# Weight pieces, x tiles and merged tiles placed at multiples of 256 bytes

## The chip, the cores and the metric

The kernel runs on one core of a Trainium2 chip. The metric is device time in microseconds (us) of one execution. Four compute engines matter here: TensorE (PE in the profile; its weight loads have a row of their own, PEld), VectorE (DVE), ScalarE (ACT) and GpSimd (POOL). SyncE (SP) issues the loads from device memory.

## The reference

Two layers, each of 256 tokens by 2048 features, all in float32. Of a layer, this is what costs time:

```python
h = jnp.einsum('bsd,dc->bsc', x, w_in)          # 2048 x 16396 columns
qa, ka, va, za, qb, kb, vb, zb, f_logit, g_logit = jnp.split(h, SPLIT_POINTS, axis=-1)
...
up_a = jnp.einsum('bsw,wd->bsd', out_a * jax.nn.silu(za), w_up_a)   # 1536 x 2048
up_b = jnp.einsum('bsw,wd->bsd', out_b * jax.nn.silu(zb), w_up_b)
gates = jax.nn.sigmoid(g_logit + b_gate)
g_a, g_b = gates[..., :D_MODEL], gates[..., D_MODEL:]
y = jnp.einsum('bsd,de->bse', g_a * up_a + g_b * up_b, w_out)       # 2048 x 2048
return layer_norm(DEEPNORM_ALPHA * x + y, ln_g, ln_b)
```

Between the projections stand two attentions of 12 heads each (one dilated with rotary positions, one with forget gates) over 256 tokens; they are small beside the projections.

## The kernel before, in words

Features lie on the 128 partitions, tokens along the free axis. To keep float32 accuracy every operand of a projection is split into two float32r parts, a high and a low one (`split`, L62: ACT writes the rounded high part, DVE the remainder). A product then takes two matmuls per contraction tile: the weights' high part against both parts of the activations (512 columns, L153), and the weights' low part against the activations' high part (256 columns, L157). The text calls these two matmuls one pair. Each matmul has a weight load of 128 columns of its own.

The work is a list of units. A unit is one tile of 128 weight columns against all 256 tokens, 16 contraction tiles long (12 for the up projections). It is cut into two pieces of 8 (or 6) contraction tiles. For each piece `load_raw` issues one load into one of 7 raw buffers, and `Piece.prep` splits it into one of 6 `w` buffers, which are used in turn; pieces are prepared about four ahead of the products.

Three kinds of activations are the moving operand of such units: `x` (L103 `x_at`), `gated` (12 tiles; the attention outputs) and `merged` (16 tiles that live in the 20 slots of 2 KB of the pool `s2`). In the units that make the attention values (`v_mm`, L328 on) the roles are turned round: slices of `x` are the stationary operand and both parts of the weights move (L340: 512 columns, L341: 256).

A layer runs in this order: 12 mixer pairs (six per attention branch; each one is six units on x for q, k and z, one value unit, and the attention of two heads, whose small products stand between the units), then units for the gates (on x) and the up projections (on gated) in turn, then 16 units of the output projection (on merged), then the normalisation, which writes x for the next layer. TensorE's program is this list in order.

Where the operands lie is what the change touches. Tiles of a pool stand one behind the other in each partition. In the built program:

- A `w` buffer holds [2, 1072] floats, that is 8576 bytes or 33.5 times 256. The first begins at byte 56576 (221 times 256), so buffers 0, 2 and 4 begin at a multiple of 256 and buffers 1, 3 and 5 lie 128 bytes behind one. The low part begins 4288 bytes (16.75 times 256) behind the high one: 192 bytes behind a multiple of 256 in buffers 0, 2, 4, and 64 behind one in 1, 3, 5. Slices of a piece are 512 bytes apart, so this holds for all of them. The text calls buffers 0, 2, 4 the even ones.
- Each x tile holds [part, contraction tile, 256 tokens] and begins at a multiple of 256. A 512-column moving operand is two runs of 1 KB, 2 KB apart.
- `gated` tiles begin at multiples of 256, and their 512 columns are one run of 2 KB.
- The tile `f_t` of 96 bytes stands in front of `s2`, so every slot of `s2`, and with them `merged`, begins 96 bytes behind a multiple of 256; the 512 columns are one run.

Of the kernel before, what the change touches and what calls it, by code (L numbers as in the profile page):

```python
# [10 lines left out]
F32 = mybir.dt.float32  # L11
F32R = mybir.dt.float32r
AF = mybir.ActivationFunctionType
ALU = mybir.AluOpType
# [4 lines left out]
S = 256  # L19
HD = 128  # L20
HEADS = 12
# [11 lines left out]
SLOT = KT // 4 * (NV + HEADS)  # L33


@with_exitstack
def trunk(ctx: ExitStack, tc: tile.TileContext, xt, w_st, w_v, w_vf, w_up, w_o,
# [17 lines left out]

# [1 line left out]
    def load_raw(ap, n):  # L57
# [8 lines left out]
    class Piece:  # L66
        """Some contraction tiles of one unit's weights."""

# [4 lines left out]
        def prep(self):  # L73
            n = len(self.kts) * self.w
            raw = load_raw(self.ap, n)
            self.t = wp.tile([128, 2, SLOT], F32R, name="w", tag="w", bufs=6)
            split(self.t[:, 0, :n], self.t[:, 1, :n], raw)
# [5 lines left out]
    class Unit:  # L83
        """One tile of weight columns against all tokens."""

# [5 lines left out]
        def cut(self, chunks):  # L91
            """Cut into pieces of the given numbers of contraction tiles."""
            self.pieces = []
            k = 0
            for n in chunks:
                self.pieces.append(Piece(self, self.ap[:, k * self.w:(k + n) * self.w], range(k, k + n), self.w))
                k += n
            self.pieces[0].first = True
            self.pieces[-1].last = True
# [3 lines left out]
    def x_at(kt):  # L103
        return xs[kt // 2][:, :, kt % 2]

    def load_x(k0, n):
        raw = load_raw(xt[:, k0:k0 + n, :].rearrange("p a b -> p (a b)"), n * S)
        for i in range(n // 2):
            x = xs[k0 // 2 + i]
            split(x[:, 0].rearrange("p a b -> p (a b)"), x[:, 1].rearrange("p a b -> p (a b)"),  # L110
                  raw[:, 2 * i * S:2 * (i + 1) * S])

# [13 lines left out]
    def keep_warm(n):  # L126
        """Products nobody reads: an idle TensorE falls to half its clock."""
        p = psc.tile([128, 2 * S], F32, name="pw", tag="po")
        for _ in range(n):
            nc.tensor.matmul(p, warm[:, :128], warm, start=True, stop=True)  # L130
# [16 lines left out]
    def stat_mm(acts, ps, kt_n, halves=2):  # L147
        """Products with both parts of the activations, and of their high part with the weights' low part."""
        def mm(kt, w):
            a = acts(kt)  # L150
            first, last, o = kt == 0, kt == kt_n - 1, ps()[:, :S]
            if halves == 2:
                nc.tensor.matmul(ps(), w[:, 0], a, start=first, stop=False)  # L153
            else:
                nc.tensor.matmul(o, w[:, 0], a[:, 0], start=first, stop=False)  # L155
                nc.tensor.matmul(o, w[:, 0], a[:, 1], start=False, stop=False)  # L156
            nc.tensor.matmul(o, w[:, 1], a[:, 0], start=False, stop=last)  # L157
        return mm

    def fold(dst, ps, scale=1.0):  # L160
        """dst = scale * (sum of the two halves of a bank)"""
        c = att.tile([128, S], F32, name="c", tag="c", bufs=3)
        nc.scalar.activation(c, ps[:, S:], AF.Copy, scale=scale)  # L163
        if scale == 1.0:
            nc.vector.tensor_tensor(dst, ps[:, :S], c, op=ALU.add)  # L165
        else:
            nc.vector.scalar_tensor_tensor(dst, ps[:, :S], scale, c, op0=ALU.mult, op1=ALU.add)

    def pair_units(aps, acts, nk, done, scale=1.0, put=None, halves=(2, 2)):
        """Two column tiles, whose results come side by side."""  # L170
        st = {}
        ps = {}

        def before(i):
            ps[i] = mm_tile()

        def after(i):
            if put:
                put(i, ps[i])
            else:  # L180
                if i == 0:
                    st["p"] = slot("p")
                fold(st["p"][:, i], ps[i], scale)
            if i == 1:
                done(st.get("p"))

        return [Unit(ap, nk, 128, stat_mm(acts, lambda i=i: ps[i], nk, halves[i]),
                     before=lambda i=i: before(i), after=lambda i=i: after(i))
                for i, ap in enumerate(aps)]

# [1 line left out]
    def build_layer(l):  # L192
# [9 lines left out]
        def forget(psv):  # L202
            f = att.tile([128, 2, HEADS], F32, name="f_t", tag="f_t", bufs=1)
            for t in range(2):
                nc.vector.tensor_copy(f[:, t], psv[t][:, NV:NV + HEADS])
            lf["f"] = f
# [31 lines left out]
        def attention(br, p, st):  # L238
            """Stages of the attention of one pair of heads."""
            hs = [dict(), dict()]  # L240
# [184 lines left out]

        # output projection, residual, statistics (of four times the residual sum)
        ln = {"s": []}

        def residual(j2):
            u = slot("u")  # L430
            r = big.tile([128, 2, S], F32, name="gated", tag="gated", bufs=HEADS)
            x = xs[j2].bitcast(F32)
            nc.gpsimd.tensor_tensor(u, x[:, 0], x[:, 1], op=ALU.add)  # L433
            if j2 == 0:
                ln["u"] = u
            else:
                nc.vector.scalar_tensor_tensor(r, u, alpha4, ln["c"][:, None, :].to_broadcast([128, 2, S]),
                                               op0=ALU.mult, op1=ALU.subtract)
            ln[j2] = r

        def add_stats(r, sl):
            """Sums over the feature tiles of the shifted values and of their squares."""
            if not ln["s"]:
                ln["s"] = [slot("lns") for _ in range(2)]
                nc.scalar.activation(ln["s"][1], r, AF.Square)
                nc.vector.tensor_copy(ln["s"][0], r)
                return
            sq = slot("sq")
            nc.scalar.activation(sq[:, sl], r[:, sl], AF.Square)
            for a, b in zip(ln["s"], (r, sq)):  # L450
                nc.vector.tensor_tensor(a[:, sl], a[:, sl], b[:, sl], op=ALU.add)

        def add_in(dst, ps):
            """dst += both halves of a bank"""
            c = att.tile([128, S], F32, name="c", tag="c", bufs=3)
            nc.scalar.activation(c, ps[:, S:], AF.Copy)
            nc.vector.tensor_tensor(dst, dst, ps[:, :S], op=ALU.add)
            nc.vector.tensor_tensor(dst, dst, c, op=ALU.add)
# [18 lines left out]
        def last_tiles():  # L477
# [3 lines left out]
            def first(ps):  # L481
                add_in(r[:, 0], ps)
                add_stats(r, slice(0, 1))
                for a in ln["s"]:
                    nc.vector.tensor_tensor(a[:, 0], a[:, 0], a[:, 1], op=ALU.add)
                # brings in the table set that the statistics need
                t = sm.tile([128, 1], F32, name="t", tag="t", bufs=1)
                nc.scalar.activation(t, ln["s"][1][:, 0, :1], AF.Sqrt)

            def second(ps):  # L490
# [3 lines left out]
                pst = psc.tile([128, 2, 2], F32, name="pst", tag="pt")  # L494
                # the sums share one bank, which the first product clears
                for n, (a, i) in enumerate([(ln["s"], 0), ((r, sq), 1)]):
# [11 lines left out]
        def spread(v, name):  # L508
            """A value per token, on every partition."""
            p = psc.tile([128, S], F32, name=name, tag="s", bufs=2)  # L510
# [30 lines left out]
        def ln_apply(j2):  # L541
            r, x = ln[j2], xs[j2]
            g, b = ([t[:, l * KT + 2 * j2 + i:l * KT + 2 * j2 + i + 1] for i in range(2)] for t in (lng, lnb))
            if j2 == 0 and not final:
                for i in range(2):
                    nc.vector.tensor_tensor(r[:, i], r[:, i], ln["pa"], op=ALU.mult)
                    nc.scalar.activation(x[:, 0, i], r[:, i], AF.Identity, scale=g[i], bias=b[i])
                    nc.vector.tensor_scalar(r[:, i], r[:, i], g[i], b[i], op0=ALU.mult, op1=ALU.add)
                    ins = nc.vector.tensor_tensor(x[:, 1, i], r[:, i], x[:, 0, i].bitcast(F32),  # L549
                                                  op=ALU.subtract)  # L550
            else:
# [11 lines left out]
                if not final:  # L563
                    nc.scalar.activation(x[:, 0], r, AF.Copy)
                    ins = nc.vector.tensor_tensor(x[:, 1], r, x[:, 0].bitcast(F32), op=ALU.subtract)
            if not final:
# [18 lines left out]

# [1 line left out]
    units, jobs, interleaved, norms = [], {}, set(), {}  # L587
# [32 lines left out]
    for g in order:  # L620
        done += len(g)
        n = number[id(g[0].unit)]
        if g[0].first and n in norms:
            # the normalisation comes before what is prepared for later
            stats, apply = norms[n]
# [105 lines left out]
```

## Time and profile before

| | |
|---|---|
| median of 3 runs | 1997.46 us (1996.6 to 1997.53) |
| the profiled execution, first to last instruction | 1996.8 us |
| PE busy | 1974.5 us (99%), 11449 matmuls |
| DVE busy | 1270.7 us (64%) |
| ACT busy | 988.3 us (49%) |
| POOL busy | 75.9 us (4%) |

The profiled execution is 0.66 us shorter than the median, so a sum made against the profile's 1996.8 us is taken to the median by adding 0.66. A matmul's duration in the profile holds its latency, and matmuls overlap; what one costs on TensorE is read from the distance of its start to the start of the next.

### The profile page before, as it was taken

To read this page: it belongs to the slowest core of one execution; us is meant where nothing else is said; L and a number is where in the kernel's file an instruction comes from. 1 tells how busy PE (TensorE), PEld (TensorE's weight loads), DVE (VectorE), ACT (ScalarE), POOL (GpSimd) and SP (SyncE) were. 2 spreads that over 40 slices of the span, in tenths; PEclk is the share of its full clock that TensorE was granted. 3 is DMA by queue.
4 is the path that set the end of the run, shared out by engine and by line. 5 is a ranking of instruction groups with operands and counts; after the bars stand their busy time and mean duration, and the time that the engine had idled before them with its cause. 6 is when DMAs were issued, how large, how long until landed. Compare 5 with 4: busy or idle time off the path is not lost.

```text
span 1996.8 us, 29718 instructions
## 1 busy us (share of the span) xinstructions
PE 1974.5 (99%) x11449; PEld 1733.9 (87%) x11449; DVE 1270.7 (64%) x1896; ACT 988.3 (49%) x1555; POOL 75.9 (4%) x69
## 2 busy tenths in 40 slices
PE   9999999999999999999999999999999999999997
PEld 7888888889888888888888888888898888888886
DVE  7666665555555555668777666655555555556686
ACT  5444445454544445554455444445454444445544
POOL 0000000001000000001200000000010000000022
PEclk9999999999999999999999999999999999999998
DMA  8655555666556555565455555566666555556651
GB/s 305 198 172 178 177 160 174 189 196 213 183 177 182 178 168 178 182 200 189 158 169 178 170 180 174 163 181 183 205 200 185 184 178 176 168 173 194 204 182 60
DMA packets 107766, 362.74 MB, mean 182 GB/s; under 512 B 12368, under 2 KB 15592, under 8 KB 107624
## 3 DMA queue, kind: packets, MB, share of 16 engines
q1 hardware_dynamic: 106600, 357.68, 57.7%
q0 software_dynamic: 1024, 3.17, 0.6%
q8 instruction: 89, 1.46, 0.3%
q14 instruction: 53, 0.43, 0.1%
HBM read 358.68 MB, written 2.12 MB: 181 GB/s over the span
## 4 chain that ended last, share of the span: by engine, by line
PE 97%; DVE 1%; DMA 1%; ACT 0%; issue 0%; DVEq 0%; ACTq 0%
PE mm L153 53%; PE mm L157 27%; PE mm L340 8%; PE mm L341 4%; PE ps_s L247 1%; PE po L276 1%; PE pt L267 1%; DMA raw<-xt 1%; PE ps_s L246 1%; PE po L277 1%; PE mm L336 0%; PE mm L337 0%; PE mm L338 0%; DVE gated L557 0%; PE mm L156 0%; PE mm L155 0%
## 5 line engine op out<-in xcount | busy, mean ns | idle before, releaser
L153 PE MATMUL mm<-x,w 128*128 128x512 f32 x3328 | 1183.4, 399 | 8.0 <-DVE x L549 4.8
L64 DVE TENSOR_TENSOR w<-raw,w 128x1024 fp32r<-128x1024 f32 (+3 forms) x713 | 839.6, 1182 | 461.7 <-ACT w L63 460.3
L63 ACT ACTIVATE w<-raw 128x1024 fp32r<-128x1024 f32 (+3 forms) x713 | 716.9, 1007 | 471.3 <-issue 225.2
L157 PE MATMUL mm<-x,w 128*128 128x256 f32 x3328 | 932.2, 280 | 0.2 <-DVE w L64 0.2
L153 PEld LDWEIGHTS mm<-x,w 128*128 128x128 f32 x3328 | 626.9, 189 | 151.6 <-issue 5.1
L157 PEld LDWEIGHTS mm<-x,w 128*128 128x128 f32 x3328 | 627.8, 189 | 2.6 <-DVE w L64 1.4
L163 ACT ACTIVATE c<-mm 128x256 f32<-128x256 f32 x320 | 122.2, 384 | 453.4 <-PE mm L157 423.8
L153 PE MATMUL mm<-gated,w 128*128 128x512 f32 x768 | 267.5, 393 | 0.0
L340 PE MATMUL mm<-w,x 128*128 128x512 f32 x704 | 245.6, 392 | 0.0
L165 DVE TENSOR_TENSOR p<-mm,c 128x256 f32<-128x256 f32 x252 | 106.6, 424 | 187.1 <-ACT c L163 186.6
L157 PE MATMUL mm<-gated,w 128*128 128x256 f32 x768 | 213.9, 279 | 0.0
L341 PE MATMUL mm<-w,x 128*128 128x256 f32 x704 | 197.0, 280 | 0.0
L153 PEld LDWEIGHTS mm<-gated,w 128*128 128x128 f32 x768 | 144.2, 188 | 32.9
L153 PE MATMUL mm<-merged,w 128*128 128x512 f32 x480 | 168.9, 395 | 0.0
L340 PEld LDWEIGHTS mm<-w,x 128*128 128x128 f32 x704 | 132.0, 187 | 29.6
L157 PEld LDWEIGHTS mm<-gated,w 128*128 128x128 f32 x768 | 143.9, 187 | 0.0
L157 PE MATMUL mm<-merged,w 128*128 128x256 f32 x512 | 143.5, 280 | 0.0
L341 PEld LDWEIGHTS mm<-w,x 128*128 128x128 f32 x704 | 132.7, 189 | 0.0
L153 PEld LDWEIGHTS mm<-merged,w 128*128 128x128 f32 x480 | 90.1, 188 | 21.6 <-DVE merged L64 0.6
L157 PEld LDWEIGHTS mm<-merged,w 128*128 128x128 f32 x512 | 96.2, 188 | 0.1
L433 POOL TENSOR_TENSOR u<-x 128x512 f32<-128x512 f32 x16 | 31.6, 1977 | 609.4 <-DVE merged L64 487.4
L256 ACT ACTIVATE z<-z,s 128x128 f32<-128x128 f32 x96 | 42.3, 444 | 0.0
(129 smaller groups left out, 939.4 us busy)
## 6 DMA issues: line engine op xcount, KB each, us to landing
raw<-w_st SPq DMA_DIRECT2D x410, 512.0 KB, 3.7
raw<-w_up SPq DMA_DIRECT2D x128, 384.0 KB, 3.2
raw<-w_v SPq DMA_DIRECT2D x88, 512.0 KB, 4.3
raw<-w_o SPq DMA_DIRECT2D x64, 512.0 KB, 3.7
raw<-w_vf SPq DMA_DIRECT2D x8, 536.0 KB, 4.0
nb<-cum POOLq DMA_DIRECT2D x12, 256.0 KB, 4.6
raw<-w_st SPq DMA_DIRECT2D x9, 256.0 KB, 5.9
yt<-gated SPq DMA_DIRECT2D x8, 256.0 KB, 2.1
```

The lines of the kernel that those rows point to most:

```text
L63: nc.scalar.activation(hi, src, AF.Copy)
L64: nc.vector.tensor_tensor(lo, src, hi.bitcast(F32), op=ALU.subtract)
L153: nc.tensor.matmul(ps(), w[:, 0], a, start=first, stop=False)
L157: nc.tensor.matmul(o, w[:, 1], a[:, 0], start=False, stop=last)
L163: nc.scalar.activation(c, ps[:, S:], AF.Copy, scale=scale)
L165: nc.vector.tensor_tensor(dst, ps[:, :S], c, op=ALU.add)
L246: nc.tensor.matmul(ps[:, 0], q[:, :128], k[:, :128], start=True, stop=True)
L247: nc.tensor.matmul(ps[:, 1:3].rearrange("p a b -> p (a b)"), q[:, 128:], k, start=True, stop=True)
L256: nc.scalar.activation(z[:, sl], z[:, sl], AF.Exp, scale=-1.0, bias=s4[:, c:c + 1], accum_out=s4[:, 2 + c:3 + c])
L340: nc.tensor.matmul(o, xh, w, start=first, stop=False)
L341: nc.tensor.matmul(o[:, :NV], xl, w[:, 0], start=False, stop=last)
L433: nc.gpsimd.tensor_tensor(u, x[:, 0], x[:, 1], op=ALU.add)
```

## The change

The low part of a `w` buffer begins `PART` = 1088 floats (4352 bytes, 17 times 256) behind the high part, and a buffer is 8704 bytes (34 times 256), so that both parts of all six buffers begin at multiples of 256. An x tile holds [contraction tile, part, 256 tokens]: it still begins at a multiple of 256, and a 512-column operand is one run of 2 KB. `f_t` is given 256 bytes, so that `s2`, and with it `merged`, begins at a multiple of 256. The stationary slices of x in the value units stay at multiples of 256. In the value units the moving weights are, as before, one run of each part.

```diff
 SLOT = KT // 4 * (NV + HEADS)
 
+PART = (SLOT + 63) // 64 * 64
...
             raw = load_raw(self.ap, n)
-            self.t = wp.tile([128, 2, SLOT], F32R, name="w", tag="w", bufs=6)
+            self.t = wp.tile([128, 2, PART], F32R, name="w", tag="w", bufs=6)
             split(self.t[:, 0, :n], self.t[:, 1, :n], raw)
...
     def x_at(kt):
-        return xs[kt // 2][:, :, kt % 2]
+        return xs[kt // 2][:, kt % 2]
...
             x = xs[k0 // 2 + i]
-            split(x[:, 0].rearrange("p a b -> p (a b)"), x[:, 1].rearrange("p a b -> p (a b)"),
-                  raw[:, 2 * i * S:2 * (i + 1) * S])
+            split(x[:, :, 0], x[:, :, 1],
+                  raw[:, 2 * i * S:2 * (i + 1) * S].rearrange("p (a b) -> p a b", a=2))
...
         def forget(psv):
-            f = att.tile([128, 2, HEADS], F32, name="f_t", tag="f_t", bufs=1)
+            f = att.tile([128, 64], F32, name="f_t", tag="f_t", bufs=1)
+            f = f[:, :2 * HEADS].rearrange("p (a b) -> p a b", a=2)
...
-            nc.gpsimd.tensor_tensor(u, x[:, 0], x[:, 1], op=ALU.add)
+            nc.gpsimd.tensor_tensor(u, x[:, :, 0], x[:, :, 1], op=ALU.add)
...
-                    nc.scalar.activation(x[:, 0], r, AF.Copy)
-                    ins = nc.vector.tensor_tensor(x[:, 1], r, x[:, 0].bitcast(F32), op=ALU.subtract)
+                    nc.scalar.activation(x[:, :, 0], r, AF.Copy)
+                    ins = nc.vector.tensor_tensor(x[:, :, 1], r, x[:, :, 0].bitcast(F32), op=ALU.subtract)
```

No instruction is added, removed or moved on any engine, and each waits for what it waited for. Fifteen ACT and fifteen DVE instructions that write x get two runs of 256 elements instead of one of 512. ACT's program at its start, before (x_81 to x_88 are the eight x tiles):

```order
L63 ACTIVATE x_81<-raw 128x512
L63 ACTIVATE w<-raw 128x256 x3
L63 ACTIVATE x_82<-raw 128x512
L63 ACTIVATE w<-raw 128x256 x3
L63 ACTIVATE x_83<-raw 128x512
```

And of the change, the same place:

```order
L65 ACTIVATE x_81<-raw 128x2x256
L65 ACTIVATE w<-raw 128x256 x3
L65 ACTIVATE x_82<-raw 128x2x256
L65 ACTIVATE w<-raw 128x256 x3
L65 ACTIVATE x_83<-raw 128x2x256
```

Only the shape of the written tile differs.

## Rows read from the trace of the kernel before

**Rows 1.** The page: busy time by engine, and the granted clock in 40 slices.

```profile
PE 1974.5 (99%) x11449; PEld 1733.9 (87%) x11449; DVE 1270.7 (64%) x1896; ACT 988.3 (49%) x1555; POOL 75.9 (4%) x69
...
PEclk9999999999999999999999999999999999999998
```

**Rows 2.** The page: the chain that ended last, shares by engine and by line.

```profile
PE 97%; DVE 1%; DMA 1%; ACT 0%; issue 0%; DVEq 0%; ACTq 0%
PE mm L153 53%; PE mm L157 27%; PE mm L340 8%; PE mm L341 4%; PE ps_s L247 1%; PE po L276 1%; PE pt L267 1%; DMA raw<-xt 1%; PE ps_s L246 1%; PE po L277 1%; PE mm L336 0%; PE mm L337 0%; PE mm L338 0%; DVE gated L557 0%; PE mm L156 0%; PE mm L155 0%
```

**Rows 3.** What TensorE waited for: us in total, times, longest.

```profile
PE mm L153 <- DVE x L549: 4.8, 1, 4.8
...
PE mm L153 <- ACT w L63: 1.2, 1, 1.2
```

**Rows 4.** Groups of matmuls by shape: count, busy us, mean ns, idle before.

```profile
L153 PE MATMUL mm<-x,w 128*128 128x512 f32 x3328 | 1183.4, 399 | 8.0 <-DVE x L549 4.8 <-ACT w L63 1.2 <-DVE x L64 1.2
...
L153 PE MATMUL mm<-gated,w 128*128 128x512 f32 x768 | 267.5, 393 | 0.0
L340 PE MATMUL mm<-w,x 128*128 128x512 f32 x704 | 245.6, 392 | 0.0
...
L153 PE MATMUL mm<-merged,w 128*128 128x512 f32 x480 | 168.9, 395 | 0.0
```

**Rows 5.** Timeline, PE, gate and up units: start us, duration us, instruction.

```profile
811.80 0.39 PE L153 MATMUL mm<-x,w 128*128 128x512 f32 x1
...
827.06 0.39 PE L153 MATMUL mm<-gated,w 128*128 128x512 f32 x1
```

**Rows 6.** Timeline, PE, just behind the normalisation between the layers.

```profile
999.04 0.63 PE L153 MATMUL mm<-x,w 128*128 128x512 f32 x1
...
1000.33 0.63 PE L153 MATMUL mm<-x,w 128*128 128x512 f32 x1
```

**Rows 7.** Windows: stretch and length us, busy us of each engine, granted PEclk, DMA.

```profile
998.30:1001.90 3.60, 3.60 (x11) 3.12 (x12) 3.60 (x6) 1.73 (x4) 2.39 (x2) 0.50 0.00 0
811.80:827.06 15.26, 15.26 (x91) 13.37 (x90) 9.22 (x14) 7.94 (x13) 0.00 (x0) 1.00 0.61 176
```

**Rows 8.** Timeline, PE, starts of pieces in one mixer pair (even, odd, even buffer).

```profile
1182.87 0.39 PE L153 MATMUL mm<-x,w 128*128 128x512 f32 x1
...
1185.67 0.39 PE L153 MATMUL mm<-x,w 128*128 128x512 f32 x1
...
1188.50 0.40 PE L153 MATMUL mm<-x,w 128*128 128x512 f32 x1
```

**Rows 9.** Timeline, PE, a value unit: an odd buffer, then an even one from 532.85.

```profile
530.79 0.39 PE L340 MATMUL mm<-w,x 128*128 128x512 f32 x1
...
532.85 0.39 PE L340 MATMUL mm<-w,x 128*128 128x512 f32 x1
...
533.20 0.39 PE L340 MATMUL mm<-w,x 128*128 128x512 f32 x1
...
535.28 0.39 PE L340 MATMUL mm<-w,x 128*128 128x512 f32 x1
```

**Rows 10.** Timeline, PE, output projection: an even buffer, then an odd one.

```profile
940.78 0.40 PE L153 MATMUL mm<-merged,w 128*128 128x512 f32 x1
...
943.60 0.39 PE L153 MATMUL mm<-merged,w 128*128 128x512 f32 x1
...
946.38 0.40 PE L153 MATMUL mm<-merged,w 128*128 128x512 f32 x1
```

**Rows 11.** The x tile's instructions: duration ns min/median/max, first and last start us, form.

```profile
L63 ACT ACTIVATE x<-raw x8: 612/630/632, 3.8 to 21.1; 128x512 fp32r<-128x512 f32 x8
...
L565 DVE TENSOR_TENSOR x<-gated,x x7: 677/685/693, 1002.5 to 1012.9; 128x512 fp32r<-128x512 f32 x7
```

**Rows 12.** Groups by shape of other ACT and DVE instructions: count, busy us, mean ns.

```profile
L303 DVE TENSOR_TENSOR uv<-p,rope_t 128x512 f32<-128x512 f32 x48 | 30.9, 685 | 0.4
...
L64 DVE TENSOR_TENSOR gated<-gt,gated 128x256 fp32r<-128x256 f32 x48 | 20.1, 418 | 0.0
...
L63 ACT ACTIVATE gated<-gt 128x256 fp32r<-128x256 f32 x48 | 19.7, 411 | 0.0
```

More of the change, by code (lines that the diff above doesn't have):

```diff
@@ L546, in ln_apply @@
                     nc.vector.tensor_tensor(r[:, i], r[:, i], ln["pa"], op=ALU.mult)
-                    nc.scalar.activation(x[:, 0, i], r[:, i], AF.Identity, scale=g[i], bias=b[i])
+                    nc.scalar.activation(x[:, i, 0], r[:, i], AF.Identity, scale=g[i], bias=b[i])
                     nc.vector.tensor_scalar(r[:, i], r[:, i], g[i], b[i], op0=ALU.mult, op1=ALU.add)
-                    ins = nc.vector.tensor_tensor(x[:, 1, i], r[:, i], x[:, 0, i].bitcast(F32),
+                    ins = nc.vector.tensor_tensor(x[:, i, 1], r[:, i], x[:, i, 0].bitcast(F32),
                                                   op=ALU.subtract)
```

## The prediction

> **What bounds the kernel now.** I read the page first. PE is busy for 1974.5 of 1996.8 us, DVE for 64% and ACT for 49%, and the granted clock is at nine tenths or more of full speed in all slices but the last [rows 1]. The chain that ended last confirms it: 97% of it is PE, nearly all in the projection matmuls of L153, L157, L340 and L341 [rows 2]. Then I asked what TensorE waits for. The longest entry is 4.8 us, once, at the normalisation between the layers; the waits for ACT's half of a piece add up to 1.2 us [rows 3]. So no transfer and no other engine sets the end. The time is the number of matmuls times what each takes when it follows the one before, and a change that moves no instruction can act only through that second factor.
>
> The groups by shape give the number: 3328 + 768 + 704 + 480 = 5280 pairs of a 512-column and a 256-column matmul on x, gated, the value units and merged [rows 4]. For the second factor I took starts from the timeline and divided by the pairs between them; a matmul's own duration (392 to 399 ns in these groups) contains latency that its neighbours overlap and is no use here.
>
> - Gate and up units: 44 pairs from 811.80 to 827.06 us, 0.3468 us each [rows 5]. This stretch contains x as moving operand (two runs) and gated (one run), and even and odd weight buffers. Nothing in it shows that one run is faster than two.
> - Mixer pairs, units on x: here the pieces do not agree. One of 8 pairs takes 2.80 us, 0.3500 each; the next takes 2.83 us, 0.3538 each [rows 8]. Others in the same mixer pair run as in rows 5. In the mixer pair that rows 8 come from, I count seven of the twelve pieces on x in such a slow pattern.
> - Value units: in an odd buffer 6 pairs take 2.06 us, 0.3433 each; in an even buffer 6 pairs take 2.08 us, 0.3467 each [rows 9].
> - Output projection: 8 pairs in an even buffer take 2.82 us, 0.3525 each; in an odd buffer 2.78 us, 0.3475 each [rows 10].
>
> The last two lines are what makes an effect of addresses credible at all: same instructions, same moving operand, and 5 ns per pair between two buffers that differ by 128 bytes. They also show how small the effect is: all patterns seen lie between 0.3433 and 0.3538.
>
> [...]
>
> **The change part by part.**
>
> *The weights' parts.* In the gate and up stretch the high and low part are 0 and 192, or 128 and 64, bytes behind a multiple of 256, and over both the pair costs 0.3468 [rows 5]. Afterwards both are at 0, for which no row exists. The nearest row is the even buffer of a value unit: there every weight load (a slice of x) begins at a multiple of 256, and so does the moving high part; only the low half of the 512 columns lies 192 behind. It takes 0.3467 [rows 9]. I take this as the price after the change for all pairs: against 0.3468 the gain is nothing. The bounds from rows: the cheapest pattern, 0.3433, would give 5280 x 0.0035 = 18 us; the dearest, 0.3538, would cost 5280 x 0.0070 = 37 us against an even 0.3468.
>
> *The x tile's order.* One run instead of two. The gate and up stretch mixes both at one price, so this alone is worth nothing there [rows 5]. The slow patterns appear only in mixer pairs, and there on x. Whether they come from the two runs, from the two kinds of buffer or from the small attention matmuls between the units no row can say. If they go, seven pieces of 8 pairs save 0.3519 (the mean of the two shown) - 0.3468 = 0.0051 us per pair, 0.286 us per mixer pair, and 6.9 us over the 24 mixer pairs. If they stay, 0. I take 6.9: if patterns arise from the relative places of two streams, one place for all leaves fewer ways to fall into one.
>
> *Merged to a multiple of 256.* Its pairs then read as gated's do. Mean now 0.3500 [rows 10]; 480 x 0.0032 = 1.5 us gained. Lower bound 0.
>
> *Writing x in two runs.* Fifteen instructions on ACT and fifteen on DVE. One ACT instruction on 512 elements takes 630 ns, on DVE 685 [rows 11]; as two separate instructions of 256 they would take 2 x 411 and 2 x 418 [rows 12], 0.19 and 0.15 us more. At most three of each stand on the chain at the start, so 1.0 us bounds it. A row with an operand whose inner runs are 256 long is L303 on DVE, at 685 ns for 512 elements [rows 12], the same as an unbroken one. I take 0.
>
> *What costs nothing.* POOL's sum of the two parts of x is read in two runs; POOL is busy 4% [rows 1]. ACT and DVE write the weights at other addresses; their idle share, 51% and 36%, covers any change there that is short of a third [rows 1]. If that cover went, PE would wait on `w` in the waits view, where 1.2 us stand now. Loads go to the same raw buffers.
>
> Sum: 1996.8 - 6.9 - 1.5 = 1988.4 us for the profiled execution. The median of the runs lies 0.66 above the profile: 1989.
>
> [...]
>
> **The rivals.**
>
> *Nothing happens.* The slow patterns come from the attention matmuls between the units, not from places, and only merged gains: 1996.8 - 1.5 = 1995.3, median 1996. For it: gate and up units, where nothing stands between the units, never show the patterns, with the same buffers and the same two runs [rows 5]. Against it: the output projection has its own slow pattern without attention [rows 10]. Chance 0.20, for a median of 1993.5 to 2001.5.
>
> [...] Chance 0.20, for a median below 1986. [...]
>
> *The slow pattern everywhere.* The same alignment for both streams may make them meet more often. If the pairs of gate, up and value units took 0.3500 as well, the mean over 5280 would rise from today's 0.3468 + 8.4/5280 = 0.3484 to 0.3500: 8.4 us more, 2005 in the profile and 2006 in the median; at 0.3538 it is 29 us more, 2026. It decides against the kernel from a mean of 0.3492 per pair on, where the loss reaches 4 us. For it: the even buffer, whose high part is at a multiple of 256, is the dearer one in both rows 9 and 10. Against it: in rows 5 it is not. Chance 0.18.
>
> **How the numbers follow.** The likeliest case, the patterns gone and the base price kept, has 0.42, with a range of its own of 1986 to 1994. A measurement of this kernel tells a change from none at about 0.2%, 4 us. Faster by more: 0.40 of the likeliest case and the 0.20 of the rival below 1986, 0.60. Within: 0.21, made of the rival "nothing happens" and the edges of the cases beside it. Slower: 0.19. The range goes down through most of the gain's cases to 1955 (leaving 0.09, the deep removals) and up to 2005 (leaving 0.10).
>
> **What would show it.** In the profile after: starts in the mixer pairs' pieces 2.77 to 2.78 us apart per 8 pairs, in the output projection 2.77 in each buffer, and in the gate and up units still 0.347 per pair. Count and order of matmuls, waits of TensorE and the clock row should stand as before. I am wrong in the base price if gate and up units move from 0.3468 in either direction: each ns there on all pairs is 5.3 us. I am wrong on the patterns if mixer pieces at 0.350 and more remain. A new wait of PE for `w` or x would be a mechanism that I don't expect.

## The result and the profile after

The median went from 1997.14 to 2016.12 us: a ratio of 1.0095, 95% interval 1.0081 to 1.0109. The change made the kernel slower by 19 us, where 8 us less were forecast. The profiled execution spans 2012.3 us. Two executions that took over twice as long as all others, the only one of e7 (4343 us, the kernel of e9, with a granted clock of 1.00) and one of e5 (4855 us), are left out of what follows, and why they were slow stays open.

The page after (busy time by engine, the granted clock in 40 slices, the chain that ended last by engine), which answers to [rows 1, 2]:

```profile
PE 1990.7 (99%) x11449; PEld 1736.6 (86%) x11449; DVE 1270.6 (63%) x1896; ACT 988.9 (49%) x1555; POOL 75.6 (4%) x69
...
PEclk9999999999999999999999999999999999999998
...
PE 98%; DVE 1%; DMA 1%; ACT 0%; issue 0%
```

The same 11449 matmuls, the same clock, the same work on DVE, ACT and POOL. PE alone is busy 16.2 us longer, a little more than the 15.5 us by which the span grew. The waits of TensorE (us in total, times, longest) are within half a microsecond those of [rows 3]:

```profile
PE mm L155 <- DVE x L552: 4.8, 1, 4.8
PE mm L155 <- ACT w L65: 1.6, 2, 1.3
```

The groups of matmuls by shape (count, busy us, mean ns of one), against [rows 4]:

```profile
L155 PE MATMUL mm<-x,w 128*128 128x512 f32 x3328 | 1191.5, 401 | 7.2 <-DVE x L552 4.8 <-ACT w L65 1.6 <-DVE x L568 0.7
...
L155 PE MATMUL mm<-gated,w 128*128 128x512 f32 x768 | 272.6, 399 | 0.0
L343 PE MATMUL mm<-w,x 128*128 128x512 f32 x704 | 249.6, 399 | 0.0
...
L155 PE MATMUL mm<-merged,w 128*128 128x512 f32 x480 | 167.8, 396 | 0.0
```

Products on gated went from 393 to 399 ns and those of the value units from 392 to 399. Only merged stayed, 395 and 396. Durations overlap: in the stretch below a 512-column product lasts 0.40 us, and the next product starts 0.24 us behind its start. So the price shows in the starts. Timeline of PE in the gate and up units (start us, duration us), against [rows 5]:

```profile
818.84 0.40 PE L155 MATMUL mm<-x,w 128*128 128x512 f32 x1
819.19 0.40 PE L155 MATMUL mm<-x,w 128*128 128x512 f32 x1
819.54 0.40 PE L155 MATMUL mm<-x,w 128*128 128x512 f32 x1
819.90 0.40 PE L155 MATMUL mm<-x,w 128*128 128x512 f32 x1
...
830.14 0.40 PE L155 MATMUL mm<-gated,w 128*128 128x512 f32 x1
```

32 pairs take 11.30 us, 0.3531 each, through x and gated and through even and odd buffers alike; by [rows 5] it was 0.3468. To the nanosecond the starts repeat every three pairs: 349, 350, 361, a mean of 353.3.

In the output projection (merged) 16 pairs take 5.54 us, 0.3463, where the even buffer had 0.3525 and the odd one 0.3475 [rows 10]:

```profile
937.84 0.39 PE L155 MATMUL mm<-merged,w 128*128 128x512 f32 x1
...
943.38 0.39 PE L155 MATMUL mm<-merged,w 128*128 128x512 f32 x1
```

Where the 15.5 us lie, by windows. The two stretches of gate and up units in a layer (the first from the last attention product to the last up unit; the second from the last attention product to the next product of another kind, which takes in the first units of the output projection), then the rest of the output projection (stretch and length us, busy us of PE, PEld, DVE, ACT, POOL with counts, granted clock, DMA):

```profile
316.36:457.81 141.45, 141.45 (x804) 122.66 (x803) 80.28 (x96) 68.99 (x102) 0.00 (x0) 1.00 0.62 188
765.01:919.96 154.95, 154.93 (x877) 133.97 (x875) 98.72 (x130) 80.07 (x126) 1.29 (x1) 1.00 0.61 189
920.28:990.87 70.59, 70.59 (x408) 61.73 (x407) 59.39 (x71) 34.55 (x45) 14.28 (x7) 1.00 0.56 183
```

Before, these lasted 138.88, 152.29 and 71.29 us. In both kernels the second layer repeats them to 0.01 us. So the gate and up stretches lost 2 x (2.57 + 2.66) = 10.5 us, the output projection gained 2 x 0.70 = 1.4, and the remaining 6.4 us were lost around the mixer pairs, where 6.9 were to be gained. Of these, 4.0 are the value units' (704 pairs at 353.1 ns instead of 347.4); the distances behind starts on x in mixer pairs sum up to 2.0 us more (887.6, before 885.6).

### The profile page after: what moved, and what is told of

Its sections match the earlier page's. It is cut to its first block, busy times and chain, and to the rows that moved or that the text cites. A ratio compares the mean times of both kernels' runs of the same rounds, so it can differ in the third digit from the quotient of the medians.

```text
span 2012.3 us, 29718 instructions
## 1 busy us (share of the span) xinstructions
PE 1990.7 (99%) x11449; PEld 1736.6 (86%) x11449; DVE 1270.6 (63%) x1896; ACT 988.9 (49%) x1555; POOL 75.6 (4%) x69
## 3 DMA queue, kind: packets, MB, share of 16 engines
q0 software_dynamic: 1024, 3.17, 0.6%
## 4 chain that ended last, share of the span: by engine, by line
PE 98%; DVE 1%; DMA 1%; ACT 0%; issue 0%
PE mm L155 53%; PE mm L159 27%; PE mm L343 8%; PE mm L344 4%; PE ps_s L250 1%; PE po L279 1%; PE pt L270 1%; DMA raw<-xt 1%; PE po L280 1%; PE ps_s L249 1%; PE mm L341 0%; PE mm L340 0%; PE mm L339 0%; DVE gated L560 0%; PE mm L158 0%; PE mm L157 0%
## 5 line engine op out<-in xcount | busy, mean ns | idle before, releaser
L155 PE MATMUL mm<-gated,w 128*128 128x512 f32 x768 | 272.6, 399 | 0.0
```

## The experiments

In the tables, a price is the mean distance in ns between the starts of neighbouring pairs, leaving out distances over 420 ns, where another product or a wait stands between, and a few under 300 at the program's start. "mixers" are the units on x in mixer pairs, "values" the value units. A ratio is against executions of the kernel before that were timed beside the run. The kernels up to e6 ask which part of the change costs; the theories are that the weights' place does it alone, because both streams begin alike ("same place"), or that the old step of 128 bytes between neighbouring buffers had kept TensorE out of a slow pattern ("kick"), or that the order of x does it ("x order").

**e1, the weights alone:** the kernel before with one line changed.

```diff
-            self.t = wp.tile([128, 2, SLOT], F32R, name="w", tag="w", bufs=6)
+            self.t = wp.tile([128, 2, PART], F32R, name="w", tag="w", bufs=6)
```

> The change's weight buffers alone (both parts of all six at multiples of 256 bytes); x in its old order, merged 96 bytes behind a multiple. Theory 'same place' (with both parts at the same place modulo 256, the load of one part and the moving columns of the other fall into the pattern of 349, 350, 361 ns, mean 353): gate and up units at 0.3533 per pair, time 2014 to 2018 us. Theory 'kick' (the slow patterns exist before and after; the old step of 128 bytes between buffers throws TensorE out of them at every other piece): the same here. Theory 'x order' (one run of 2 KB for x is what makes it slow): gate and up units stay at 0.3468, time 1996 to 1999 us.

**e2, all but the weights:** the changed kernel with that line undone.

> x in its new order and merged at multiples of 256, weight buffers as before. 'Same place' and 'kick' both: gate and up units 0.3468 per pair, output projection under 0.3480 in both kinds of buffer, time 1989 to 1997 us depending on whether the mixer pieces' slow patterns go. 'x order': 0.353 in gate units on x, time above 2008 us.

**e3 and e4, other places of the parts,** in the changed kernel: high at 0 and low at 192 in all six buffers (e3), and both parts at 0 in even and at 128 in odd buffers (e4, which has 2208 and `2 * PART` where e3's diff has 2176 and `2 * SLOT`).

```diff
-            self.t = wp.tile([128, 2, PART], F32R, name="w", tag="w", bufs=6)
+            self.t = wp.tile([128, 2176], F32R, name="w", tag="w", bufs=6)
+            self.t = self.t[:, :2 * SLOT].rearrange("p (a b) -> p a b", a=2)
```

> As the changed kernel, but the low part begins 4288 bytes behind the high one again: in all six buffers the high part is at a multiple of 256 and the low part 192 behind one, and no step of 128 between buffers is left. 'Same place': gate and up units fall back to 0.3468, time 1988 to 1998 us. 'Kick': a slow pattern, once entered in a mixer pair, stays through the pieces behind it, mean of gate and up units 0.350 or more, time 2006 us or more.

> As the changed kernel, but a buffer is 8832 bytes: both parts of a buffer lie at the same place modulo 256, at 0 in buffers 0, 2, 4 and at 128 in 1, 3, 5, so the step of 128 between buffers is back. 'Same place': still 0.3533 in gate and up units, time 2010 to 2018 us. 'Kick': 0.3468 in gate and up units, time 1990 to 1999 us.

**e5 and e6, two parts of the change at a time:** weights and x with the old `f_t` of 96 bytes (e5), weights and the new `f_t` with the old x (e6).

> Weights and x as in the changed kernel, merged (and all tiles of its pool) 96 bytes behind a multiple. Alone, the weights cost nothing and the two other parts cost nothing, so the loss is in a combination. Theory 'pairing of weights and x': gate, up and value units at 0.351 or more per pair, time 2008 us or more. Theory 'history' (which of several patterns runs is set by what interrupted TensorE last, and is carried on through units whose own operands would allow a faster one): any value between 1994 and 2016 us, and gated units, whose operands are those of the weights-only kernel, need not stay at its 0.3467.

> Weights and merged at multiples of 256, x in its old order. 'Pairing of weights and x': 0.3467 in gate, up and value units, output projection under 0.348, time 1991 to 1997 us. 'History': the attention's operands move with merged's pool, so the starting conditions differ from those of the weights-only kernel; any value between 1990 and 2016 us.

| | median us | ratio, 95% | gated | values | mixers | merged |
|---|---|---|---|---|---|---|
| before | 1997.14 | | 346.5 | 347.4 | 349.4 | 350.2 |
| changed | 2016.12 | 1.0095 (1.0081 to 1.0109) | 353.3 | 353.1 | 351.3 | 347.6 |
| e1 | 1996.89 | 0.9995 (0.9986 to 1.0005) | 346.7 | 347.0 | 348.9 | 350.2 |
| e2 | 1995.37 | 0.9988 (0.9978 to 0.9997) | 346.7 | 347.9 | 349.1 | 347.1 |
| e3 | 2001.71 | 1.0021 (1.0011 to 1.0030) | 350.0 | 346.7 | 349.4 | 348.5 |
| e4 | 2010.70 | 1.0065 (1.0049 to 1.0080) | 351.9 | 351.6 | 350.3 | 351.9 |
| e5 | 1995.35 | 0.9991 (0.9981 to 1.0001) | 346.7 | 347.0 | 348.9 | 350.2 |
| e6 | 2015.81 | 1.0090 (1.0073 to 1.0107) | 353.3 | 353.1 | 351.3 | 350.2 |

e1 refutes that the weights' place costs by itself: with both parts of all buffers at multiples of 256 the products on gated stand at 346.7. The loss of the 128-byte step, which is gone there too, costs nothing by itself either. Of the two other placements, e3 has the price that "kick" foresaw (350.0) but not its time (2006 us or more), e4 the time of "same place" but not its price (353.3). e5 against e6 clears the order of x. What costs is the weights' places together with the 96 or 256 bytes of `f_t`. That is odd: the gate and up units read weights, x and gated, and none of them moved between e1 (346.7 on gated) and e6 (353.3). What stands behind `f_t` are merged and, in the same pool, the operands of the attention products. The groups of e5, then of e6:

```profile
L155 PE MATMUL mm<-gated,w 128*128 128x512 f32 x768 | 267.5, 391 | 0.0
```

```profile
L155 PE MATMUL mm<-gated,w 128*128 128x512 f32 x768 | 272.6, 399 | 0.0
```

The operands of these products lie at the same addresses, at 391 and 399 ns. So a price is not a property of the operands in the row.

The changed kernel shows it within one trace, in the output projection, around two small products of the statistics:

```profile
912.71 0.39 PE L155 MATMUL mm<-merged,w 128*128 128x512 f32 x1
...
919.42 0.40 PE L155 MATMUL mm<-merged,w 128*128 128x512 f32 x1
919.96 0.70 PE L472 MATMUL pc<-gated,ones 128*128 128x256 f32 x2
...
920.85 0.40 PE L155 MATMUL mm<-merged,w 128*128 128x512 f32 x1
...
925.70 0.40 PE L155 MATMUL mm<-merged,w 128*128 128x512 f32 x1
```

Ahead of them 19 pairs take 6.71 us, 0.3532 each; behind them 14 take 4.85, 0.3464 each. Moving operand and weights begin at multiples of 256 on both sides.

The next theory, "history" (its rival, "operands", has the price fixed by where the operands lie): TensorE has several steady patterns of starts, the last interruption decides which one it lands in, and it can stay there until the next. The interruption ahead of a gate and up stretch is an attention, whose operands lie in that pool.

**e10 and e11, the pool moved on:** the changed kernel with `f_t` of 128 and of 192 bytes, so that the pool begins 128 or 192 behind a multiple of 256. The diff is that of e10; e11 has 48.

```diff
-            f = att.tile([128, 64], F32, name="f_t", tag="f_t", bufs=1)
+            f = att.tile([128, 32], F32, name="f_t", tag="f_t", bufs=1)
```

> The changed kernel with the pool of merged and of the attention's operands 128 bytes behind a multiple of 256; weights, x and gated stay at multiples. Theory 'history' (the attention's operands decide in which pattern TensorE leaves each attention job): gate and up units, which read nothing from this pool, still change their price, to 0.3467 if the jobs leave it in the fast pattern; time then 1989 to 1999 us, else 2010 to 2018 us. Theory 'operands': gate and up units stay at 0.3533.

> The same with the pool 192 bytes behind a multiple of 256. 'History': one of the same two outcomes, not necessarily the same as at 128. 'Operands': gate and up units stay at 0.3533.

e10 took 2014.69 us (ratio 1.0089, 1.0073 to 1.0104), gated at 353.3. e11 took 2003.87 (1.0032, 1.0018 to 1.0046), gated at 346.7, merged (now at +192) at 353.2. The timeline of e11 in a gate and up stretch:

```profile
818.10 0.40 PE L155 MATMUL mm<-x,w 128*128 128x512 f32 x1
...
829.19 0.40 PE L155 MATMUL mm<-gated,w 128*128 128x512 f32 x1
```

32 pairs in 11.09 us, 0.3466 each, with operands that all lie where the changed kernel has them. The place of a pool that TensorE doesn't read in these units changes their price: on gated 353.3 with the pool at 0 or 128, 346.7 with it at 192. ACT and DVE do write into that pool meanwhile (gate and up results, merged), so e10 and e11 alone can't tell the attention ahead from these writes; e13 can.

**e8 and e9, added interruptions:** before every second unit of the gate and up stretches one product on constants, 64 to 512 columns in turn, 56 in all, whose result nobody reads; in the kernel before (e8) and in the changed one (e9).

```diff
+    def kick():
+        n = sizes[len(kicks) % 8]
+        kicks.append(n)
+        p = psc.tile([128, 2 * S], F32, name="kick", tag="po")
+        nc.tensor.matmul(p[:, :n], warm[:, :128], warm[:, :n], start=True, stop=True)
...
+            for u in range(g0 + 4, len(units), 2):
+                at(u, kick)
```

> The kernel before with the same 56 extra products. If operands set the price, 0.3467 stays in gate and up units. 'History': behind some of the extra products units run at 0.350 or 0.353.

> [...] Theory 'operands': 0.3533 per pair stays in gate and up units, time 2016 to 2024 us. Theory 'history': behind some sizes of extra product whole units run at 0.3467 with unchanged operands, so the mean of gate and up units lies between, near 0.350, and the time is under 2014 us although there are 56 products more.

e9 took 2015.67 us (1.0093, 1.0073 to 1.0113), more than the 2014 that "history" allowed; a single execution of e8 took 2012.26. In e9, around a product of 256 columns (PE's timeline):

```profile
817.18 0.40 PE L164 MATMUL mm<-gated,w 128*128 128x512 f32 x1
...
820.01 0.40 PE L164 MATMUL mm<-gated,w 128*128 128x512 f32 x1
820.25 0.28 PE L168 MATMUL mm<-gated,w 128*128 128x256 f32 x1
820.36 0.28 PE L143 MATMUL kick<-warm 128*128 128x256 f32 x1
820.48 0.40 PE L164 MATMUL mm<-x,w 128*128 128x512 f32 x1
...
821.19 0.39 PE L164 MATMUL mm<-x,w 128*128 128x512 f32 x1
...
823.27 0.39 PE L164 MATMUL mm<-x,w 128*128 128x512 f32 x1
```

Ahead of it 8 pairs take 2.83 us, 0.3538 each; two pairs behind it 6 take 2.08, 0.3467 each. In e9 what follows four of the sizes is the same from stretch to stretch: behind each of the seven products of 192 columns the price is 353.3, behind each of 256 it falls from 353.3 to 346.7, behind 320 and 384 it is 346.7. Behind 64, 448 and 512 columns it was 353.3 once each and 346.2 to 346.7 the other times. In e8 gated rises to 349.8 in the mean and the gate units from 347.4 to 350.6 (without the distances that hold an added product): the kernel before has slow patterns for these units too, and without the products does not land in them. In e8 the pattern also changes inside a unit, from one buffer to the next, with parts at 350 to 353; in the gate and up units of e9, at 353.3 or 346.2 to 346.7, it does not. Each product costs some 30 ns (64 columns) to 235 ns (512) itself, 56 of them 7.3 us, and this eats in e9 what the faster pairs give back.

**e12 and e13, the changed kernel with a few such products:** one of 256 columns in each of the four stretches (e12, the first added line), four of 320 columns in each (e13, the other two).

```diff
+            at(len(units) + 4, kick)
...
+            for u in (4, 6, 8, 10):
+                at(len(units) + u, kick)
```

> The changed kernel with four extra products that nobody reads, of 256 columns each, one in front of the first up unit of each of the four gate and up stretches. In the run with 56 such products this size was always followed by the fast pattern. Behind each stand 28 units, 384 pairs. 'History': they go from 0.3533 to 0.3467 per pair; 1536 pairs save 10.2 us, the four products cost 0.12 us each, so the time falls by about 9.7 us, to 2006 us (2003 to 2009). 'Operands': 0.3533 stays, and the time is the changed kernel's plus 0.5 us, 2016 us.

> The changed kernel with extra products of 320 columns in front of the first, second, third and fourth pair of units behind the first gate units of each of the four gate and up stretches (16 in all). Four products of 256 columns at the first of these places left the slow pattern as it was; in the run with 56 products, 320 columns always had the fast pattern behind them, and where the fast one ran already it stayed. 'History': in each stretch one of the four places catches the slow pattern and from there on the pairs run at 0.3467, so gate and up units average 0.348 to 0.351; up to 1536 pairs save 6.7 ns, the 16 products cost 0.15 us each, 2.4 us: 2006 to 2011 us. 'Operands': 0.3533 stays throughout, 2018 us.

e12 missed its forecast of 2003 to 2009 us: 2014.81 us (1.0086, 1.0069 to 1.0103), 353.3 ahead of the product and behind it, in four of four stretches. The size alone doesn't decide; the product came at another unit than those of 256 columns in e9, and whether the phase of the three-pair cycle is what differs I did not separate. e13 took 2008.93 (1.0063, 1.0046 to 1.0080). Its timeline at the first such product of a stretch:

```profile
765.43 0.40 PE L159 MATMUL mm<-x,w 128*128 128x512 f32 x1
...
768.26 0.40 PE L159 MATMUL mm<-x,w 128*128 128x512 f32 x1
768.61 0.31 PE L138 MATMUL kick<-warm 128*128 128x320 f32 x1
768.76 0.39 PE L159 MATMUL mm<-gated,w 128*128 128x512 f32 x1
...
771.53 0.39 PE L159 MATMUL mm<-gated,w 128*128 128x512 f32 x1
```

8 pairs in 2.83 us before, 8 in 2.77 us behind, and so in all four stretches: gated stands at 346.73 in the mean. 768 pairs on gated at 6.6 ns less and 1024 gate pairs on x at 5.0 less (352.9 to 347.9) make 10.2 us, less 16 x 0.14 for the products and 1.2 for merged, which landed at 350.1, 6.8; measured were 7.2. Most of the gate and up loss is undone by adding work, with every operand, and every write of ACT and DVE, where the change put it. This shows that at unchanged places what ran before sets the price.

**e14, a map of places:** in the changed kernel each mixer pair has another place of the two parts, all 16 combinations of 0, 64, 128 and 192 bytes; the other units keep 0 and 0.

```diff
+            self.t = wp.tile([128, 2304], F32R, name="w", tag="w", bufs=6)
+            hi, lo = self.unit.place
+            self.t = self.t[:, hi:hi + 2 * (PART + lo - hi)].rearrange("p (a b) -> p a b", a=2)
...
+                        u.place = (c % 4 * 16, c // 4 % 4 * 16)
```

> The changed kernel with the high part 0, 64, 128 or 192 bytes and the low part 0, 64, 128 or 192 bytes behind a multiple of 256, another of the 16 combinations in each mixer pair (24 pairs; gate, up and output units and the value unit with the forget gates at 0 and 0). If places alone set a price, each combination shows one price per pair and repeats it where it comes twice; if history picks among several, one combination shows two or more within a mixer pair, at 0.3467 and 0.3533 and little between. No forecast of the time beyond 1990 to 2020 us.

A single execution took 2007.77 us. Prices of the units on x in ns (0, 0 from the second of its two mixer pairs, as the first stands at the program's start, between waits):

| high part at | low at 0 | 64 | 128 | 192 |
|---|---|---|---|---|
| 0 | 351.3 | 346.8 | 350.1 | 351.1 |
| 64 | 346.5 | 352.7 | 351.6 | 352.2 |
| 128 | 351.9 | 346.9 | 350.9 | 350.1 |
| 192 | 345.4 | 348.3 | 347.0 | 352.6 |

The diagonal, both parts at one place as in the change, holds the two dearest and averages 351.9, the other cells 349.0. The rest follows no rule that I can state. Seven cells besides 0, 0 come twice: five repeat their mean within 0.2 ns, two differ by about 1. So with the same work in between, the place sets most of a cell's mean. But a mean can hold several patterns: in the cells 192, 0 and 64, 0 some units run at 340, cheaper than any steady pattern before, and others at 350.

**e15, e16, e17, three cells everywhere** (all units but the one for the forget gates): high 192 and low 0, high 64 and low 0, high 0 and low 64. **e18:** the first of them in the kernel before, with its old x and `f_t`. Places are in floats; e16 has (16, 0), e17 (0, 16).

```diff
+            self.place = (48, 0) if w <= NV else (0, 0)
```

> The changed kernel with all weight pieces at one unequal pair of places: high part 192 bytes behind a multiple of 256, low part at a multiple (the pieces of the unit with the forget gates stay at 0 and 0). In the map the mixer units on x averaged 0.3455 here, with pairs of 0.340 and 0.350, against 0.3524 at 0 and 0. Theory 'equal places open the slow pattern': no 0.353 cycle anywhere, mean over all pairs 0.3455 to 0.3470, time 1981 to 1991 us, faster than before and after. Theory 'history alone': the places don't matter, any mean between 0.3467 and 0.3520, 1990 to 2016 us.

> The same with the high part 64 bytes behind a multiple and the low part at one. Map: 0.3466 in mixer units on x, again with pairs of 0.340. 'Equal places': mean over all pairs 0.3460 to 0.3475, 1984 to 1993 us. 'History alone': 1990 to 2016 us.

> The same with the high part at a multiple and the low part 64 bytes behind one. Map: 0.3469 in mixer units on x, but 0.3533 in the value units, where the weights move. 'Equal places': units on x, gated and merged at 0.3469, value units at up to 0.3533, 1990 to 1996 us. 'History alone': 1990 to 2016 us.

> The kernel before with nothing changed but the places of the weights: high part 192 bytes behind a multiple of 256, low part at one, in all six buffers; x keeps its old order, merged and the attention operands stay at +96. If the weights' places set which patterns are possible, and x order and the pool only help to choose among them, the 340 ns pattern is there again: gate and up pairs at 340, time 1967 to 1975. If the attention operands' place decides whether the 340 pattern is entered (as it decided between 346.7 and 353.3), the gate and up pairs stand at 346.7 or 350 and the time is 1990 to 2000. If the order of x or merged carried the gain, likewise 1990 or more.

| | median us | ratio, 95% | gated | values | mixers | merged |
|---|---|---|---|---|---|---|
| e15 | 1969.47 | 0.9861 (0.9846 to 0.9876) | 340.0 | 347.2 | 343.2 | 340.2 |
| e16 | 1995.77 | 0.9994 (0.9984 to 1.0003) | 350.0 | 346.8 | 346.8 | 346.0 |
| e17 | 1993.72 | 0.9982 (0.9973 to 0.9992) | 346.7 | 353.2 | 346.9 | 346.7 |
| e18 | 1973.86 | 0.9881 (0.9865 to 0.9898) | 340.0 | 347.2 | 343.3 | 353.3 |

e15 beats both kernels, by over 11 us more than its forecast; e16 stands 3 us above its own, e17 in it. Its longer buffers are not the reason: e14's gate and up units, in buffers of the same length with both parts at 0, have 353.3 on gated. In the mixers, e16 and e17 come close to the map (346.8 and 346.9 against 346.5 and 346.8); e16's gate and up units landed in the pattern of 350 that its cell also showed there. The page of e15, and then PE's timeline, in the gate and up units and in the output projection:

```profile
PE 1946.1 (99%) x11449; PEld 1721.9 (87%) x11449; DVE 1271.3 (65%) x1896; ACT 988.7 (50%) x1555; POOL 76.2 (4%) x69
```

```profile
763.64 0.39 PE L158 MATMUL mm<-x,w 128*128 128x512 f32 x1
...
774.52 0.39 PE L158 MATMUL mm<-gated,w 128*128 128x512 f32 x1
...
924.63 0.39 PE L158 MATMUL mm<-merged,w 128*128 128x512 f32 x1
...
930.07 0.39 PE L158 MATMUL mm<-merged,w 128*128 128x512 f32 x1
```

The same 11449 matmuls keep PE busy 28.4 us less than before. 32 gate and up pairs take 10.88 us and 16 merged pairs 5.44, both 0.3400 each. In e18, with merged at +96:

```profile
924.66 0.40 PE L158 MATMUL mm<-merged,w 128*128 128x512 f32 x1
...
930.32 0.40 PE L158 MATMUL mm<-merged,w 128*128 128x512 f32 x1
```

16 pairs take 5.66 us, 0.3538 each. The other prices of e15 and e18 are alike. So the cheap pattern, 340.0 on gated in both, needs neither the new x nor the new `f_t`; and here the place of a moving operand decides at once: the pairs on gated stand at 340 up to the last, and those on merged behind them, with no attention between, at 353.

## Why the prediction was wrong, point by point

**What bounds the kernel** held: PE alone, no new wait, the second factor alone moved.

**The weights' parts** is the step that failed. "I take this as the price after the change for all pairs: against 0.3468 the gain is nothing": the price became 0.3533 on gated, 0.3531 in the value units, the gate and up stretches lost 10.5 us and the value units 4.0. The working took the even buffer of a value unit for the nearest row and so treated a price as a property of where operands lie. e5, e6, e10, e11 and e13 show that at the same places it is 346.7 or 353.3, by what interrupted TensorE last (e13 and the pairs on merged around 919.96), and that moving a pool can change it. Even had I had a row with both parts at 0, it could have read either; e1 gives the forecast's own 346.7. The bound of 37 us at 0.3538 held; that 19 us came, the middle of it, is chance.

**The x tile's order** failed in sign. The slow mixer patterns were to go, 6.9 us gained; 6.4 us were lost around the mixer pairs. 4.0 of these are the value units', so they belong to the step above; about 2.0 are lost on x, whose pairs went from 349.4 to 351.3, and not by the order: e6, with the old x, has the same 351.3 there, and e2, with the new x and the old weights, 349.1. The reason I gave, that one place for all leaves fewer ways into a pattern, is the reverse of e14's diagonal. That the order itself is worth nothing in the gate and up units was right (e5, e6).

**Merged** came out in the number, 1.5 us forecast and 1.4 found in its windows, and in e2, which has it without the weights and gained 0.12%, about 2 us. The reason did not hold in the changed kernel: its pairs were to read as gated's do, and gated reads 353.3 there, merged 347.6. The same places gave 353.2 ahead of the small products at 919.96, 346.4 behind them and 350.1 in e13, so the landing was luck.

**Writing x in two runs, and what costs nothing:** right; ACT 988.9, DVE 1270.6, PE's wait for `w` 1.6 us.

**The rivals.** "The slow pattern everywhere" is what happened, at 2016 between its two prices of 2006 and 2026. The evidence held against it, that rows 5 don't show the slow pattern in even buffers, was one landing of a system with several: in e8 the same units of the kernel before, in even and odd buffers, run in part at 350 to 353. "Nothing happens" needed the patterns to come from attention rather than places. Places matter (340.0 on gated in e15, 353.3 in the changed kernel), and so does what ran before (at unchanged places gated has 353.3 in the changed kernel and 346.7 in e13). The 0.20 for a median below 1986, and with it the range down to 1955, counted on equal places giving back a large part of the price, which no run shows: with both parts at multiples of 256 the lowest median is 1995.35 (e5). Unequal places gave 1969.47, with 6.5 ns less per pair on gated than before (340.0 against 346.5, e15).

By placement alone the times lie between 0.9861 (e15) and 1.0095 (the changed kernel) of the kernel before, and the cheapest steady pattern of any run is 0.340 us per pair (e15, e18).

**What stays open:** what in the chip makes the patterns; which of the attention products, and what of them, decides the landing; and whether 256 bytes is the measure of place that counts, since no run moved one part alone by a whole 256.

## What to carry to other kernels

Where TensorE is 99% busy with back-to-back float32r pairs, the price per pair moved here by 4% (340 to 353 ns) by where operands lie, and at unchanged places by what ran just before (on gated 353.3 in the changed kernel, 346.7 in e13): read it from starts, stretch by stretch, and don't carry it from one stretch to another. An equal alignment of all streams is not a safe choice: it took 2016.12 us here, against 1997.14. Place both parts of the weights by a map like e14, then time the best cells in the whole kernel, since a cell's mean can hold several patterns and other units may land in a dearer one, as in e16 (350.0 on gated, where the map's mixer units had 346.5). Changes of layout anywhere in a pool can move a stretch whose matmuls don't read it (gated at 353.3 in e10, at 346.7 in e11), so a 1% change after one is no proof that the edited part did it.

## What was not expected of the hardware

- Steady prices stand at a few levels: 340.0 ns (e15), 346.7 (e1), 350.0 (e3, e16) and 353.3 (the changed kernel), on gated.
- They repeat: the two gate and up stretches last 141.45 and 154.95 us in layer one and the same to 0.01 us in layer two; and in e9 the same pattern follows each of the seven products of a size: 353.3 behind 192 columns, 346.7 behind 256, 320 and 384.
- In the changed kernel a pattern lives on through changes of moving operand, buffer and unit, for over 150 us: starts 349, 350 and 361 ns apart from 765.01 to 919.42.
